# Two transformer blocks on one core: pulls joined, latent norms spread, combination weights in one tile, keys and first queries turned during dense work, and a last product with tokens on partitions

## The chip, the cores and the metric

The program runs on one core of a Trainium2 chip. The metric is the device time of one execution in microseconds (us), the median over several runs. TensorE (PE, with PEld for its weight loads), VectorE (DVE), ScalarE (ACT) and GpSimd (POOL) each take instructions in order from a queue of their own; SyncE (SP) issues most of the transfers.

## What is computed

512 tokens of width 1024 in float32 go through two kinds of block. The first block has two layers. A layer projects the normed input to twelve parts and mixes them three ways (latent attention, gated linear attention in chunks, retention in chunks), adds the output projection, and then a feed-forward part with a convolution over three tokens:

```
x = x + concat([y_a, y_b, y_c], axis=-1) @ w_out[l]
h = rmsnorm(x, ffn_norm[l]); u = h @ ffn_w_up[l]
x = x + (silu(causal_dwconv(a, ...)) * bv) @ ffn_w_down[l]
```

The second block has one layer with three branches: windowed attention in three dilated groups of eight heads, whose outputs are combined by a softmax over the groups' log-denominators; grouped-query attention with eight query heads and two key heads (RMS norm and rotation of queries and keys); and attention to 256 memory tokens. Each branch is gated, projected and merged, and the end is

```
out = merged @ w_out[layer]
x = x + rms_norm(out, g_post[layer])
```

## The kernel before

Features lie on partitions and tokens along the free axis (`x` is 128 x 8 x 512), so that a dense product is a sequence of matmuls with 512 token columns. For accuracy both operands of a dense product are split into a high and a low part (`split`, `split_weight`), and `mm3` issues three matmuls for one: high by high, high by low, low by high (lines 444 to 446). `dense` gives features on partitions (tile `ps`, 512 columns), `dense_tok` tokens on partitions (tile `pt`, 256 columns). Weights arrive in 326 pieces of up to 512 KB over SP's queue (`load`, three buffers), and each is split on ACT (line 424) and DVE (line 425), one piece ahead of its use.

The order of the work is set by a queue of generators, the class `Fill`. `fill.add` appends dense work; `f(us)`, that is `pull`, runs generators until about that many nominal us of dense work have been issued; `after(us, fn)` has a function run when so much more dense work has gone by; `settle` runs everything that is due or will be; `need(name)` runs the queue until that name is done. The pulls stand between the steps of an attention or mixing stage, so that PE has dense work while DVE and ACT prepare the next step. Their sizes stand in `PACE`. The tile framework's planner then places the instructions of each engine, so the trace does not follow the written order everywhere. PSUM has eight banks: three for dense work (`bank`) and five for all else (`mbank`). Most scratch tiles come from one ring of 43 buffers (`gt`).

The places that the change touches:

`later_rstd` computes the norms of the two latent projections (tiles `Rq`, `Rk`). `first` sums the squares through transposes and runs an inverse root of ten small DVE operations (`rsqrt`, line 500 its last); `second`, due `PACE["rank2"]` later, spreads the result over partitions by four small matmuls (`rows`, line 529). `uq_dense` calls `settle` before it reads them.

`gla` works through eight levels of block sizes (32, 16, 8, 4, 2, 1, 0, 64). At each level every head's small tiles of scores go into a PSUM bank of their own (tile `lv`, line 858, row groups of 32 and a column position of their own), with a pull after each of four token tiles; then ACT or DVE copies them on (`gD`, `gA`). `mix_out` multiplies the scores `A` with the values (tile `o`, line 912) and adds the state's part (line 907), for `gla` and for `ret`. `ret` makes its scores head by head (tile `rsc`, line 968), each followed by a DVE product (`rA`) and a pull.

In the second block `combine` turns the statistics of the three window groups (`stat`), makes the weights on DVE, puts a high and a low part into `cF`, turns it (tile `cf`, line 1425) and spreads it by matmuls (`cw`). `gqa_dense` projects and rotates queries (`bo`) and keys (`bk`, POOL line 1516); `gqa` then turns keys and queries on PE (`bkp`, `bqp`), splits them and runs the score loop (`bs`, line 1571). `finish` computes the last product with features on partitions, in two halves of 256 tokens, takes the norm over partitions through transposes (`tsq`) and row matmuls (`rows`), adds `x` and writes the output transposed; the host turns it back. A matmul in plain float32 leaves two records in the trace, a transpose one.

Of the kernel before, what the change touches and what calls it, by code (L numbers as in the profile page):

```python
# [17 lines left out]
S = 512  # L18
# [10 lines left out]
    rank2=6.0,  # L29
# [52 lines left out]
def weight_groups():  # L82
# [72 lines left out]
    two("out", "w_out_2", k8, _span(0, 1024))  # L155
# [180 lines left out]
class Prog:  # L336
# [74 lines left out]
    def split_weight(self, i):  # L411
# [362 lines left out]
    def gla(self, l, bc):  # L774
# [60 lines left out]
        for li, hs in enumerate(seq):  # L835
# [16 lines left out]
            for t in range(4):  # L852
# [7 lines left out]
                f(PACE["gla"])  # L860
# [36 lines left out]
    def mix_out(self, l, gkey, nkey, A, v, st, qg, bc, b0):  # L897
# [40 lines left out]
    def ret(self, l, bc, late, more):  # L938
# [185 lines left out]
    def run(self):  # L1124
# [11 lines left out]
        if self.stop:  # L1136
            nc.sync.dma_start(self.aps["out"].rearrange("(k p) t -> p k t", p=128), self.x)
            return
# [4 lines left out]
    def block2(self):  # L1143
# [14 lines left out]
        og, st = [], []  # L1158
        for gi in range(3):
# [22 lines left out]
        for i in range(4):  # L1182
            fill.add(("br", 2, i), self.branch(2, i, opm))
        fill.need()
# [97 lines left out]
    def window(self, gi):  # L1282
# [8 lines left out]
        st = self.cst1.tile([128, 4, 16], F32, name="stat", tag="stat", bufs=6)  # L1291
# [89 lines left out]
    def combine(self, og, st):  # L1381
        nc, T4, f = self.nc, self.T4, self.f
        scale = 64 ** -0.5
        for gi in (1, 2):
# [9 lines left out]
            st[gi] = self.cst1.tile([128, 4, 16], F32, name="stat", tag="stat", bufs=6)  # L1394
            nc.scalar.activation(st[gi], pb, AF.Copy)
# [345 lines left out]
```

## Time and profile before

| | us |
|---|---|
| median of 3 runs | 1990.25 (1987.42 to 1991.47) |
| profiled execution | 1990.08 |
| its span, first to last instruction | 1988.3 |
| PE busy in the span | 1954.8 (98%) |
| DVE busy | 1239.2 (62%) |
| ACT busy | 793.4 (40%) |
| POOL busy | 140.7 (7%) |

The profile is of one execution. An engine's busy time is the union of its instructions' spans. Matmuls are pipelined, so that a span reaches into the next one's: the time that a matmul adds is the distance from its start to the next start. The mean granted clock of TensorE is 0.993 of full speed.

### The profile page before, as it was taken

The page shows a single profiled execution, that of the slowest core. Times are in us where ns is not written, and L with a number is a line of the kernel's source. Part 1 is how long each engine was busy: PE and PEld are TensorE (multiplying, and loading weights), DVE is VectorE, ACT ScalarE, POOL GpSimd, SP SyncE. Part 2 cuts the span into 40 slices and gives each one's busy share as a digit, 9 for nine tenths or more (in the row PEclk, how much of TensorE's full clock was granted, in tenths as well). Part 3 has the DMA queues.
Part 4 walks back from the last instruction along what each step waited for, and adds up shares of the span by engine and source line. Part 5 has one row for each costly group of instructions (what it writes and reads, how often), then busy time and mean ns, then how long its engine had stood idle before and what let it go on. Part 6 is the DMA issues. An engine that isn't in the chain of part 4 may idle for free.

```text
span 1988.3 us, 28658 instructions
## 1 busy us (share of the span) xinstructions
PE 1954.8 (98%) x11351; PEld 1620.4 (81%) x11351; DVE 1239.2 (62%) x2299; ACT 793.4 (40%) x1473; POOL 140.7 (7%) x172
## 2 busy tenths in 40 slices
PE   9999999999999999999999999999999999999997
PEld 7879888888888878888888888887888877788887
DVE  6666576646556666576656466845456787655454
ACT  5545243222224635443222224525354456543242
POOL 1000000000000100000000000021131330000000
PEclk9999999999999999999999999999999999999998
DMA  5221123232323321133232334432222221123331
GB/s 196 60 80 44 64 89 101 84 109 85 106 80 107 94 67 50 41 96 95 93 90 96 103 113 123 135 109 67 75 75 67 75 64 54 63 67 98 101 96 54
DMA packets 55189, 172.30 MB, mean 87 GB/s; under 512 B 6494, under 2 KB 10096, under 8 KB 55056
## 3 DMA queue, kind: packets, MB, share of 16 engines
q1 hardware_dynamic: 53152, 165.47, 26.6%
q0 software_dynamic: 1760, 4.87, 0.9%
q8 instruction: 89, 1.46, 0.3%
q14 instruction: 44, 0.36, 0.1%
q10 hardware_dynamic: 144, 0.14, 0.0%
HBM read 167.05 MB, written 2.10 MB: 85 GB/s over the span
## 4 chain that ended last, share of the span: by engine, by line
PE 91%; DVE 5%; ACT 3%; issue 1%; POOL 0%; DMA 0%; DVEq 0%; POOLq 0%; ACTq 0%
PE ps L444 24%; PE ps L446 23%; PE ps L445 23%; PE pt L444 3%; PE pt L445 3%; PE pt L446 3%; PE o L912 2%; DVE wlo L425 1%; PE o L1029 1%; PE s L1006 1%; PE aq L1347 1%; PE bo L1596 1%; PE bpq L1584 1%; PE rows L529 1%; PE lv L858 1%
## 5 line engine op out<-in xcount | busy, mean ns | idle before, releaser
L424 ACT ACTIVATE whi<-wst 128x1024 fp32r<-128x1024 f32 (+3 forms) x318 | 316.3, 995 | 700.3 <-PE ps L445 566.4
L425 DVE TENSOR_TENSOR wlo<-wst,whi 128x1024 fp32r<-128x1024 f32 (+3 forms) x318 | 367.4, 1155 | 315.9 <-ACT whi L424 315.4
L444 PE MATMUL ps<-xh,whi 128*128 128x512 f32 (+1 forms) x1408 | 556.8, 396 | 0.0
L445 PE MATMUL ps<-xl,whi 128*128 128x512 f32 (+1 forms) x1408 | 550.3, 391 | 0.6 <-DVE xl L490 0.6
L446 PE MATMUL ps<-xh,wlo 128*128 128x512 f32 (+1 forms) x1408 | 549.8, 391 | 0.1
L444 PEld LDWEIGHTS ps<-xh,whi 128*128 128x128 f32 (+1 forms) x1408 | 264.4, 188 | 61.1 <-issue 6.7
L446 PEld LDWEIGHTS ps<-xh,wlo 128*128 128x128 f32 (+1 forms) x1408 | 264.3, 188 | 57.1 <-DVE wlo L425 0.9
L445 PEld LDWEIGHTS ps<-xl,whi 128*128 128x128 f32 (+1 forms) x1408 | 264.6, 188 | 55.8 <-DVE xl L490 2.8
L444 PE MATMUL pt<-whi,xh 128*128 128x256 f32 x480 | 143.2, 299 | 1.5 <-ACT bz L1523 0.8
L445 PE MATMUL pt<-wlo,xh 128*128 128x256 f32 x480 | 137.6, 287 | 0.0
L445 PE MATMUL ps<-fl,whi 128*128 128x512 f32 x352 | 137.0, 389 | 0.0
L444 PE MATMUL ps<-fh,whi 128*128 128x512 f32 x352 | 137.0, 389 | 0.0
L446 PE MATMUL ps<-fh,wlo 128*128 128x512 f32 x352 | 136.9, 389 | 0.0
L446 PE MATMUL pt<-whi,xl 128*128 128x256 f32 x480 | 136.5, 286 | 0.0
L444 PEld LDWEIGHTS pt<-whi,xh 128*128 128x128 f32 x480 | 92.7, 194 | 6.7 <-ACT bz L1523 1.3
L1067 DVE TENSOR_TENSOR x<-x,ps 128x512 f32<-128x512 f32 x96 | 65.7, 687 | 50.8 <-PE ps L446 50.6
L445 PEld LDWEIGHTS pt<-wlo,xh 128*128 128x128 f32 x480 | 93.3, 194 | 0.5 <-issue 0.2
L446 PEld LDWEIGHTS pt<-whi,xl 128*128 128x128 f32 x480 | 92.9, 194 | 0.2 <-issue 0.2
L445 PEld LDWEIGHTS ps<-fl,whi 128*128 128x128 f32 x352 | 66.1, 188 | 13.8
L446 PEld LDWEIGHTS ps<-fh,wlo 128*128 128x128 f32 x352 | 66.1, 188 | 13.7
L444 PEld LDWEIGHTS ps<-fh,whi 128*128 128x128 f32 x352 | 66.1, 188 | 13.6
L486 ACT ACTIVATE fh<-cv 128x512 fp32r<-128x512 f32 x44 | 27.9, 633 | 84.7 <-DVE cv L1121 84.7
(464 smaller groups left out, 2919.1 us busy)
## 6 DMA issues: line engine op xcount, KB each, us to landing
wst<-in_w SPq DMA_DIRECT2D x250, 512.0 KB, 3.5
wst<-in_w SPq DMA_DIRECT2D x54, 384.0 KB, 3.0
wst<-in_w SPq DMA_DIRECT2D x20, 256.0 KB, 2.6
x<-in_xT SPq DMA_DIRECT2D x8, 256.0 KB, 4.9
out<-out SPq DMA_DIRECT2D x8, 256.0 KB, 2.3
mt<-in_memT POOLq DMA_DIRECT2D x4, 256.0 KB, 4.1
c<-in_cst POOLq DMA_DIRECT2D x3, 256.0 KB, 3.5
s<-in_cst POOLq DMA_DIRECT2D x3, 256.0 KB, 2.9
```

The costliest lines, as they stand in the source:

```text
L424: nc.scalar.activation(hi, s3, AF.Copy)
L425: nc.vector.tensor_sub(lo, s3, hi.bitcast(F32))
L444: nc.tensor.matmul(out, lh, rh, start=start, stop=False, skip_group_check=True)
L445: nc.tensor.matmul(out, lh, rl, start=False, stop=False, skip_group_check=True)
L446: nc.tensor.matmul(out, ll, rh, start=False, stop=stop, skip_group_check=True)
L486: nc.scalar.activation(hi, src, AF.Copy)
L529: nc.tensor.matmul(ps[:, t, :], w, self.ident, start=True, stop=True)
L858: nc.tensor.matmul(ps[h][j0:j0 + w, t, c0:c0 + w], ke[hp, a:a + w], qe[hp, a + off:a + off + w], start=True, stop=True, tile_position=(32 ...
L912: nc.tensor.matmul(o[r, j, hd], A[h][:n, t, r], v[t][:n, hd], start=t + h == 0, stop=True, skip_group_check=True)
L1006: nc.tensor.matmul(s[:, :nk], qn[h][:, T4[qt]], kn[h][:, :nk], start=False, stop=True, skip_group_check=True)
L1029: nc.tensor.matmul(O[qt][:, h, :], PT[u][:, T4[kt]], v[kt][:, T4[h]], start=kt == 0, stop=kt == qt)
L1067: nc.vector.tensor_add(xm, xm, ps)
```

## The change

It has these parts. (1) The second step of the latent norms is due 11 instead of 6 us after the first. (2) In `gla` the four pulls of a level become one of four times the size, after all four token tiles; in `ret` the scores of the four heads go to four banks at once, token tile by token tile with the heads innermost, and the pulls are joined. (3) `mix_out` issues the state's products first, and each product of scores and values takes all 128 rows, for the left and the right 64 score columns in turn. (4) `combine` keeps the three groups in one tile and works on all at once. (5) Keys are doubled on POOL (each key head twice), turned and split from `gqa_dense`, 4 and 9 us of dense work later, and the first query pair 12 later; the others are turned from inside the score loop; four pulls of 0.88 at the head of `gqa` go. (6) The last product has tokens on partitions: 512 output features per matmul, the first half for four token tiles at once, the second tile by tile; the norm is then one value per partition. `x` is turned in place by `residual`, which stands in the queue between two steps of the last branch. The output is written as it is.

```diff
-    rank2=6.0,
+    rank2=11.0,
...
-    two("out", "w_out_2", k8, _span(0, 1024))
+    for i in range(2):
+        g.append(((2, "out", i), "w_out_2", 0, k8, _span(512 * i, 512)))
...
-            hi, lo = (TileList([self.gt(n, (128, 2, 256), F32R) for _ in range(2)], 2) for n in ("oh", "ol"))
-            for j in range(2):
-                self.split(hi.tiles[j], lo.tiles[j], s3[:, 2 * j:2 * j + 2])
+            hi, lo = ([self.gt(n, dtype=F32R) for _ in range(kt)] for n in ("oh", "ol"))
+            for j in range(kt):
+                self.split(hi[j], lo[j], s3[:, j])
...
-                f(PACE["gla"])
+            f(4 * PACE["gla"])
...
+            first = True
             for j in range(2):
                 t = 2 * tp + j
-                sl = slice(t * 128, t * 128 + 128)
                 if t:
-                    nc.tensor.matmul(o[:, j], qg[:, sl], st[t], start=j == 0, stop=True, skip_group_check=True)
+                    nc.tensor.matmul(o[:, j], qg[:, t * 128:t * 128 + 128], st[t], start=first, stop=True,
+                                     skip_group_check=True)
+                    first = False
+            for j in range(2):
+                t = 2 * tp + j
                 for h in range(4):
                     hd = slice(64 * h, 64 * h + 64)
-                    for n in (64, 128):
-                        r = slice(n - 64, n)
-                        nc.tensor.matmul(o[r, j, hd], A[h][:n, t, r], v[t][:n, hd], start=t + h == 0, stop=True,
+                    for r in (slice(0, 64), slice(64, 128)):
+                        nc.tensor.matmul(o[r, j, hd], A[h][:, t, r], v[t][:, hd], start=False, stop=True,
...
+        ps = [self.mbank("rsc", (128, 4, 128)) for _ in range(4)]
+        for t in range(4):
+            for h in range(4):
+                hp = slice(32 * h, 32 * h + 32)
+                nc.tensor.matmul(ps[h][:, t, :], rk[hp, T4[t]], rq[hp, T4[t]], start=True, stop=True)
         for h in range(4):
-            hp = slice(32 * h, 32 * h + 32)
-            ps = self.mbank("rsc", (128, 4, 128))
-            for t in range(4):
-                nc.tensor.matmul(ps[:, t, :], rk[hp, T4[t]], rq[hp, T4[t]], start=True, stop=True)
             a = self.gt("rA", (128, 4, 128))
-            nc.vector.tensor_mul(a, ps, rd[:, h:h + 1, :].to_broadcast([128, 4, 128]))
+            nc.vector.tensor_mul(a, ps[h], rd[:, h:h + 1, :].to_broadcast([128, 4, 128]))
             A.append(a)
-            f(PACE["ret2"])
+        f(4 * PACE["ret2"])
...
+            if i == 1:
+                fill.add("res", self.residual())
...
+        M, L = self.stats[:, :, :, :8], self.stats[:, :, :, 8:]
+        F = self.gt("cF", (128, 4, 4, 32))
+        nc.gpsimd.memset(F, 0.0)
+        E, W = (self.gt(n, (128, 4, 4, 8))[:, :3] for n in ("cE", "cW"))
         mx = self.small("cmx", (4, 8))
-        nc.vector.tensor_max(mx, st[0][:, :, :8], st[1][:, :, :8])
-        nc.vector.tensor_max(mx, mx, st[2][:, :, :8])
-        E = []
-        for gi in range(3):
-            e = self.small("ce", (4, 8))
-            nc.vector.tensor_sub(e, st[gi][:, :, :8], mx)
-            nc.scalar.activation(e, e, AF.Exp, scale=scale)
-            E.append(e)
+        nc.vector.tensor_max(mx, M[:, 0], M[:, 1])
+        nc.vector.tensor_max(mx, mx, M[:, 2])
+        nc.vector.tensor_sub(E, M, mx[:, None].to_broadcast([128, 3, 4, 8]))
+        nc.scalar.activation(E, E, AF.Exp, scale=scale)
+        f(PACE["com2"])
+        nc.vector.tensor_mul(W, E, L)
         den = self.small("cden", (4, 8))
-        f(PACE["com2"])
-        for gi in range(3):
-            t = den if gi == 0 else self.small("ct", (4, 8))
-            nc.vector.tensor_mul(t, E[gi], st[gi][:, :, 8:])
-            if gi:
-                nc.vector.tensor_add(den, den, t)
+        nc.vector.tensor_add(den, W[:, 0], W[:, 1])
+        nc.vector.tensor_add(den, den, W[:, 2])
         nc.vector.reciprocal(den, den)
-        F = self.gt("cF", (128, 4, 128))
-        nc.gpsimd.memset(F, 0.0)
-        for gi in range(3):
-            nc.vector.tensor_mul(E[gi], E[gi], den)
-            hi = self.spool.tile([128, 4, 8], F32R, name="ch", tag="ch", bufs=2)
-            nc.vector.tensor_copy(hi, E[gi])
-            nc.vector.tensor_copy(F[:, :, 32 * gi:32 * gi + 8], hi.bitcast(F32))
-            nc.vector.tensor_sub(F[:, :, 32 * gi + 8:32 * gi + 16], E[gi], hi.bitcast(F32))
+        nc.vector.tensor_mul(E, E, den[:, None].to_broadcast([128, 3, 4, 8]))
+        H = self.gt("cH", (128, 4, 4, 8), F32R)[:, :3]
+        nc.vector.tensor_copy(H, E)
+        Fg = F.rearrange("p t g d -> p g t d")
+        nc.vector.tensor_copy(Fg[:, :3, :, :8], H.bitcast(F32))
+        nc.vector.tensor_sub(Fg[:, :3, :, 8:16], E, H.bitcast(F32))
+        F = F.rearrange("p t g d -> p t (g d)")
         f(PACE["com3"])
...
+        kh, kl, qT = [], [], {}
+        kd = [self.gt("bkd", (128, 4, 2, 64)) for _ in range(2)]
+
+        def doubled():
+            for s in range(2):
+                nc.gpsimd.tensor_copy(kd[s], k[:, :, None, 64 * s:64 * s + 64].to_broadcast([128, 4, 2, 64]))
+
+        def keys():
+            for s in range(2):
+                pk = self.mbank("bkp")
+                for t in range(4):
+                    nc.tensor.transpose(pk[:, T4[t]], kd[s][:, t].rearrange("p w d -> p (w d)"), self.ident)
+                kh.append(self.gt("bkh", dtype=F32R))
+                kl.append(self.gt("bkl", dtype=F32R))
+                self.split(kh[s], kl[s], pk)
+
+        def queries(u):
+            qT[u] = [self.gt("bqT", dtype=F32R) for _ in range(2)]
+            pb = self.mbank("bqp")
+            for t in range(4):
+                nc.tensor.transpose(pb[:, T4[t]], q[u // 2][t // 2][:, t % 2, T4[u % 2]], self.ident)
+            self.stack(qT[u], pb)
+        self.fill.after(4.0, doubled)
+        self.fill.after(9.0, keys)
+        self.fill.after(12.0, lambda: queries(0))
+        self.z["b"] = kh, kl, qT, v, queries
...
-        pk = self.mbank("bkp")
-        for t in range(4):
-            nc.tensor.transpose(pk[:, T4[t]], k[:, t], self.ident)
-        kh = [self.gt("bkh", dtype=F32R) for _ in range(2)]
-        kl = [self.gt("bkl", dtype=F32R) for _ in range(2)]
-        for s in range(2):
-            a, b = slice(64 * s, 64 * s + 64), slice(64 - 64 * s, 128 - 64 * s)
-            nc.scalar.activation(kh[s][a], pk[a], AF.Copy)
-            nc.scalar.activation(kh[s][b], pk[a], AF.Copy)
-            nc.vector.tensor_sub(kl[s][a], pk[a], kh[s][a].bitcast(F32))
-            nc.vector.tensor_sub(kl[s][b], pk[a], kh[s][a].bitcast(F32))
-        qT = [[self.gt("bqT", dtype=F32R) for _ in range(2)] for _ in range(4)]
-        for u in range(4):
-            pb = self.mbank("bqp")
-            for t in range(4):
-                nc.tensor.transpose(pb[:, T4[t]], q[u // 2][t // 2][:, t % 2, T4[u % 2]], self.ident)
-            self.stack(qT[u], pb)
-            f(PACE["gqa1"])
...
+        def ahead(i, u):
+            if u[0] < 3 and u[1:] == (0, 2):
+                queries(u[0] + 1)
         units = [(pr, s, t) for pr in range(4) for s in range(2) for t in range(4)]
-        self.skew(units, ((0, score), (5, turn), (6, value)), PACE["gqa2"])
+        self.skew(units, ((0, ahead), (0, score), (5, turn), (6, value)), PACE["gqa2"])
...
+    def residual(self):
+        nc = self.nc
+        self.xt = self.x.rearrange("p (a b) s -> p a (b s)", b=2).rearrange("p a (t c) -> p a t c", t=4)
+        for kp in range(4):
+            ps = [self.mbank("xT", (128, 2, 2, 128)) for _ in range(2)]
+            for t in range(4):
+                for b in range(2):
+                    nc.tensor.transpose(ps[t // 2][:, t % 2, b], self.x[:, 2 * kp + b, self.T4[t]], self.ident)
+            for j in range(2):
+                nc.scalar.activation(self.xt[:, kp, 2 * j:2 * j + 2], ps[j].rearrange("p t b c -> p t (b c)"), AF.Copy)
+            yield 0.9
...
+        g = []
+        for c in range(2):
+            t = self.gt("gpost")
+            src = self.aps["gpost"]
+            nc.gpsimd.dma_start(t, bass.AP(tensor=src.tensor, offset=src.offset + 512 * c, ap=[[0, 128], [1, 512]]))
+            g.append(t)
         for k in range(8):
             self.split(self.xh[:, k], self.xl[:, k], self.merged[k], 0.5)
...
+        ss = self.small("oss", (4, 2))
+        y = {}
+
+        def ev(t, c, ps):
+            sq = self.gt("osq2")
+            nc.scalar.activation(sq, ps, AF.Square, accum_out=ss[:, t, c:c + 1])
+            y[t, c] = self.gt("oy2")
+            nc.vector.tensor_mul(y[t, c], ps, g[c])
+
+        ps = [self.bank("ps") for _ in range(3)] + [self.mbank("po")]
+        for k0, kt, hi, lo in self.weights((2, "out", 0)):
+            for k in range(kt):
+                for t in range(4):
+                    self.mm3(ps[t], self.xh[:, k0 + k, T4[t]], self.xl[:, k0 + k, T4[t]], hi[k], lo[k],
+                             k0 + k == 0, k0 + k == 7)
+        for t in range(4):
+            ev(t, 0, ps[t])
+        kept = list(self.weights((2, "out", 1)))
+        for t in range(4):
+            ps = self.mbank("po")
+            for k0, kt, hi, lo in kept:
+                for k in range(kt):
+                    self.mm3(ps, self.xh[:, k0 + k, T4[t]], self.xl[:, k0 + k, T4[t]], hi[k], lo[k],
+                             k0 + k == 0, k0 + k == 7)
+            ev(t, 1, ps)
+            v = self.small("ov", (1,))
+            nc.vector.tensor_reduce(v, ss[:, t], AX, OP.add)
+            r = self.rsqrt(v, "ort", (1,))
+            for c in (1, 0):
+                o = y[t, c].rearrange("p (a b) -> p a b", a=2)
+                nc.vector.scalar_tensor_tensor(o, o, r, self.xt[:, 2 * c:2 * c + 2, t], op0=OP.mult, op1=OP.add)
+                (nc.sync if c else nc.scalar).dma_start(self.aps["out"][T4[t], 512 * c:512 * c + 512], y[t, c])
```

## Rows read from the trace of the kernel before

**Rows 1.** The page, chain that ended last: shares by engine.
```profile
PE 91%; DVE 5%; ACT 3%; issue 1%; POOL 0%; DMA 0%; DVEq 0%; POOLq 0%; ACTq 0%
```

**Rows 2.** Timeline of PE: start us, span us, engine, line, operation, out<-in, shape, count.
```profile
1926.81 0.39 PE L445 MATMUL ps<-opl,whi 128*128 128x512 f32 x1
1927.04 0.39 PE L446 MATMUL ps<-oph,wlo 128*128 128x512 f32 x1
1927.26 0.28 PE L444 MATMUL ps<-xh,oh 128*128 128x256 f32 x1
1927.38 0.28 PE L445 MATMUL ps<-xl,oh 128*128 128x256 f32 x1
...
1974.57 0.28 PE L446 MATMUL ps<-xh,ol 128*128 128x256 f32 x1
```

**Rows 3.** Waits of PE: line, releaser, us in total, times, longest.
```profile
PE rows L529 <- DVE Rqt L500: 4.0, 2, 2.0
PE bs L1571 <- DVE bqT L762: 3.9, 1, 3.9
...
PE rows L529 <- DVE st L893: 2.4, 2, 1.2
PE cf L1425 <- DVE cF L1421: 2.1, 1, 2.1
```

**Rows 4.** Windows: us, busy of PE, PEld, DVE, ACT, POOL, granted clock, DMA.
```profile
45.00:122.30 77.30, 72.92 (x913) 58.85 (x911) 54.09 (x121) 39.26 (x86) 11.04 (x20) 0.98 0.24 69
660.00:740.00 80.00, 75.60 (x920) 61.23 (x918) 54.73 (x124) 38.97 (x85) 11.37 (x20) 0.96 0.24 72
1603.00:1619.00 16.00, 12.13 (x54) 9.73 (x53) 14.40 (x18) 7.36 (x13) 3.34 (x2) 0.79 0.39 125
```

**Rows 5.** Timeline of PE in mix_out, first call, first half.
```profile
122.36 1.61 PE L912 MATMUL o<-tv,gA 128*64 128x64 f32 x12 [0.16 <-ACT gA L863]
123.90 0.70 PE L907 MATMUL o<-st,qg 128*128 128x256 f32 x2
124.53 1.61 PE L912 MATMUL o<-tv,gA 64*64 64x64 f32 x12
126.07 0.50 PE L444 MATMUL ps<-ckh,whi 128*128 128x512 f32 x1
```

**Rows 6.** Timeline of PE at a value product of the window stage.
```profile
1542.12 1.09 PE L1369 MATMUL ao<-apt,av 128*64 128x128 f32 x16
1543.14 0.38 PE L444 MATMUL pt<-whi,xh 128*128 128x256 f32 x1
```

**Rows 7.** Timeline of PE at two groups of level tiles in gla.
```profile
50.76 0.75 PE L858 MATMUL lv<-qe,ke 32*32 32x32 f32 x64
51.44 0.50 PE L445 MATMUL ps<-xl,whi 128*128 128x512 f32 x1
...
86.12 0.37 PE L858 MATMUL lv<-qe,ke 32*64 32x64 f32 x16
86.42 0.39 PE L444 MATMUL pt<-whi,xh 128*128 128x256 f32 x1
```

**Rows 8.** Timeline of PE at retention scores.
```profile
202.66 1.71 PE L968 MATMUL rsc<-rT 32*128 32x128 f32 x16
204.30 0.39 PE L444 MATMUL pt<-whi,xh 128*128 128x256 f32 x1
```

**Rows 9.** Timeline of PE and DVE: query transposes, and the tail.
```profile
1607.06 1.03 PE L1558 MATMUL bqp<-c_ident,bo 128*128 128x128 f32 x8
1607.85 0.48 PE L444 MATMUL ps<-xh,whi 128*128 128x512 f32 x1
...
1979.06 1.20 PE L529 MATMUL rows<-c_ident,rt 128*128 128x128 f32 x4 [2.78 <-DVE rt L500]
1980.29 1.88 DVE L1700 TENSOR_TENSOR out<-out,rows 128x512 f32<-128x512 f32 x3 [1.38 <-PE rows L529]
```

**Rows 10.** Timeline of POOL at the end of the keys' rotation.
```profile
1579.67 1.28 POOL L1516 TENSOR_TENSOR bk<-bk,bsq 128x512 f32<-128x512 f32 x1 [0.26 <-DVE bsq L1514]
```

More of the change, by code (lines that the diff above doesn't have):

```diff
@@ L1136, in run @@
         if self.stop:
-            nc.sync.dma_start(self.aps["out"].rearrange("(k p) t -> p k t", p=128), self.x)
+            nc.sync.dma_start(self.aps["out"].rearrange("t (k p) -> p k t", p=128), self.x)
             return
@@ L1158, in block2 @@
         og, st = [], []
+        self.stats = self.cst1.tile([128, 3, 4, 16], F32, name="stats")
         for gi in range(3):
@@ L1290, in window @@
             og = [self.gt("og") for _ in range(4)]
-        st = self.cst1.tile([128, 4, 16], F32, name="stat", tag="stat", bufs=6)
+        st = self.stats[:, 0] if gi == 0 else self.cst1.tile([128, 4, 16], F32, name="stat", tag="stat", bufs=2)
         mx, sm = st[:, :, :8], st[:, :, 8:]
@@ L1393, in combine @@
                 nc.tensor.transpose(pb[:, t, :], r[:, T4[t]], self.ident[:16, :16])
-            st[gi] = self.cst1.tile([128, 4, 16], F32, name="stat", tag="stat", bufs=6)
-            nc.scalar.activation(st[gi], pb, AF.Copy)
+            nc.scalar.activation(self.stats[:, gi], pb, AF.Copy)
             f(PACE["com1"])
+        M, L = self.stats[:, :, :, :8], self.stats[:, :, :, 8:]
+        F = self.gt("cF", (128, 4, 4, 32))
+        nc.gpsimd.memset(F, 0.0)
+        E, W = (self.gt(n, (128, 4, 4, 8))[:, :3] for n in ("cE", "cW"))
@@ L1541, in gqa @@
         self.fill.settle()
[L1542 to L1560 removed]
+        kh, kl, qT, v, queries = self.z["b"]
         scale = 64 ** -0.5
@@ L1663, in cross @@
         return res
-    def finish(self):
-        nc = self.nc
+    def residual(self):
[9 more added lines that the diff above has]
+            yield 0.9
@@ L1667, in finish @@
+    def finish(self):
+        nc, T4 = self.nc, self.T4
+        g = []
[4 more added lines that the diff above has]
+            g.append(t)
         for k in range(8):
             self.split(self.xh[:, k], self.xl[:, k], self.merged[k], 0.5)
-        kept = {}
-        for half in range(2):
-            tk = slice(256 * half, 256 * half + 256)
-            acc = self.gt("acc")[:, :256]
-            out = [self.gt("out", (128, 2, 256)) for _ in range(4)]
-            for i in range(4):
-                if half == 0:
-                    kept[i] = list(self.weights((2, "out", i)))
-                ps = [self.bank("ps", (128, 256)) for _ in range(2)]
-                for k0, kt, hi, lo in kept[i]:
-                    for m in range(2):
-                        sl = slice(m * 128, m * 128 + 128)
-                        for k in range(kt):
-                            self.mm3(ps[m], hi[:, k, sl], lo[:, k, sl], self.xh[:, k0 + k, tk], self.xl[:, k0 + k, tk],
-                                     k0 + k == 0, k0 + k == 7)
-                for m in range(2):
-                    n = 2 * i + m
-                    if n == 0:
-                        nc.scalar.activation(acc, ps[m], AF.Square)
-                    else:
-                        q = self.gt("sq")[:, :256]
-                        nc.scalar.activation(q, ps[m], AF.Square)
-                        nc.vector.tensor_add(acc, acc, q)
-                    nc.scalar.activation(out[i][:, m], ps[m], AF.Copy, scale=self.vec("g_post_2", n))
-            v = self.tok_sums(acc, 1, 2)
-            nc.vector.tensor_scalar(v, v, 1.0 / D, EPS, op0=OP.mult, op1=OP.add)
-            r = self.rsqrt(v, "rt", (2, 1))
-            R = self.rows(r, 2)[:, :256]
-            dst = self.aps["out"].rearrange("(i k p) t -> i p k t", i=4, k=2)
-            for i in range(4):
-                o = out[i]
-                nc.vector.tensor_mul(o, o, R[:, None, :].to_broadcast([128, 2, 256]))
-                (nc.vector if i else nc.gpsimd).tensor_add(o, o, self.x[:, 2 * i:2 * i + 2, tk])
-                nc.sync.dma_start(dst[i][:, :, tk], o)
@@ L1716, in arrays_of @@
     a["qkn"] = np.stack([q, q[sw], k, k[sw]])
+    a["gpost"] = np.ascontiguousarray(inputs["g_post_2"])
     a["mla_out"] = np.ascontiguousarray(inputs["mla_out_norm"])
@@ L1735 @@
         aps[name] = nc.dram_tensor(f"in_{name}", a.shape, F32, kind="ExternalInput").ap()
-    aps["out"] = nc.dram_tensor("out_0", (D, S), F32, kind="ExternalOutput").ap()
+    aps["out"] = nc.dram_tensor("out_0", (S, D), F32, kind="ExternalOutput").ap()
     with tile.TileContext(nc) as tc:
@@ L1739 @@
     r = run_bass_kernel_spmd(nc, [{f"in_{k}": v for k, v in arrays.items()}], core_ids=[0])
-    return np.ascontiguousarray(r.results[0]["out_0"].T)[None]
+    return np.ascontiguousarray(r.results[0]["out_0"])[None]
```

2 lines of the change are left out of this document (removed).

## Prediction

> **What bounds the kernel now.** I read the chain of waits first: 91% of it is PE [rows 1]. PE's busy share says little beyond that, since a matmul's span overlaps its successor's; look at start-to-start times instead. A matmul of 512 columns starts 0.22 to 0.23 us after the one before it, one of 256 columns 0.12 [rows 2], though their own spans are 0.39 and 0.28. Time is won on PE in three ways: fewer or better packed starts, no wait in front of a start, no stretch at half clock. So I read next what PE waits for [rows 3], then the granted clock by stage [rows 4], and then the spacing inside each group of small matmuls that the diff touches [rows 5 to 8]. The dense work is a fixed sum: a pull that moves changes what it hides, not how much there is. The sum is made against the profiled execution's 1990.1 us (span 1988.3), 0.2 us from the median shown.
>
> **mix_out, full-height products.** Today products over 64 rows alternate with products over 128. Twenty-four of their records (a float32 matmul leaves two) and two state records fill 122.36 to 126.07; less the 0.63 between 123.90 and 124.53, that is 3.08 us, 0.128 each [rows 5]. Four token tiles, four heads, two halves and two records make 64 in each of four calls: 256 x 0.128 = 32.9 us. Afterwards all products have 128 rows and write the two column halves in turn. The nearest row is the window's value product, 128 rows by 64 columns in alternating halves: 16 records from 1542.12 to 1543.14, 0.064 each, with 128 moving columns where mix_out has 64 [rows 6]. So the bounds are 0.064 (gain 16.4) and half of it (gain 24.7). I take 21, nearer the middle, because the moving columns are halved and the weight load is not. That the narrower products of rows 5 lie farther apart than those of rows 6 is what a cost between two shapes looks like. [...]
>
> **gla, joined levels.** Sixteen small tiles take 0.30 us until dense work goes on (86.12 to 86.42); 64 in one go take 0.68 (50.76 to 51.44), 0.0107 each [rows 7]. So a split costs 0.30 - 16 x 0.0107 = 0.13 us beyond its tiles. The trace has 27 such groups a layer, where the new code makes eight: 19 x 2 x 0.13 = 5 as the low bound. The high bound is 11, a little over twice that, for the late start of the dense work on either side and for fragments of two to four tiles. I take 8. The level's DVE and ACT work is hidden by one stretch of 4 x 1.3 us of dense work instead of four of 1.3.
>
> **ret, four score banks.** The products of one head lie in the same 32 rows and run one by one: 16 records from 202.66 to 204.30, 0.10 each, 64 in all, 6.6 us [rows 8]. With heads innermost, neighbours lie in different rows. Bounds: 0.064 as in rows 6 (gain 2.5), or the spacing of rows 7 scaled from 32 to 128 columns, 0.043 (gain 3.9). I take 3.5. The four DVE products that follow now start together, under the joined 4 us of pulls.
>
> **rank2, 6 to 11.** PE waits 4.0 us for Rqt and, before the second norm's rows, 2.4 us behind the states' step on DVE, each once a layer and at most 2.0 [rows 3]. Five more us of dense work go ahead of the rows, more than the longest wait, so 6.4 go. [...] Bounds 6 and 11.1; I take 10. Nothing is late next: uq settles the queue before it reads either norm.
>
> **combine in one tile.** Some 23 small DVE operations become ten; PE waits 2.1 us for the last of them [rows 3]. Bounds 0 and 2.1; I take 1.5, since weight splits stay in DVE's queue.
>
> **Keys and first queries early.** The wait of 3.9 us before the first score goes [rows 3], and with it the slow stretch, 0.79 over 16 us, 3.4 us [rows 4]. Added are two POOL copies and four transposes, 0.4 us at 0.10 each (eight from 1607.06 to 1607.85 [rows 9]). POOL ends the rope of bk at 1580.95 and that operation takes 1.28 [rows 10]; two copies of that length end near 1583.5, while the key transposes come 9 us of dense work after the projection, near 1581. If they wait, all of PE's queue waits behind them, 0 to 2.6 us; I take 1.3. The later query turns ride in the score loop. Gain 3.9 + 3.4 - 0.4 - 1.3 = 5.6; bounds 1 (the copies are late and the clock falls all the same) and 7.
>
> **finish, tokens on partitions.** 384 matmuls of 256 columns run from 1927.26 to 1974.57, 47.3 us with the norm's products between them [rows 2]. 192 of 512 columns at 0.225 take 43.2: 4.1 gained. The tail from 1974.57 to 1988.3 is 13.7 us. From it go the row products, 1979.06 to 1980.29 (1.2), and six of eight DVE operations of 512 columns, three of which take 1.88 (3.8) [rows 9]; the root's chain and the last write stay: 5.0 gained. The residual is turned on PE: 32 transposes at 0.10, 3.2, and eight switches, 4 in all. Its eight ACT copies and the loads of g_post lie under dense work of the last branch and the first output half; without that cover the copies cost PE what ACT needs beyond the transposes, some 2. The weight splits of the second half run ahead under the first. Net 4.1 + 5.0 - 4 = 5.1; bounds 1 (copies and splits show) and 7.
>
> **Sum.** 21 + 8 + 3.5 + 10 + 1.5 + 5.6 + 5.1 = 54.7; 1990.1 - 54.7 = 1935.4 us. All low bounds (16.4, 5, 2.5, 6, 0, 1, 1) give 1958, all high ones (24.7, 11, 3.9, 11.1, 2.1, 7, 7) 1923.
>
> **Rivals.**
> One half at a time: if the column halves of mix_out don't run side by side, the spacing is twice that of rows 6, 0.128, which is today's; the 21 go, 1956. For it: both halves use all rows. Against: rows 6. Chance 0.12.
> Cover runs out: DVE or ACT come last in the mixing stages. DVE is busy 54.1 of 77.3 us in the first one [rows 4]; with 4 us less of small tiles and 5 less of waits and half clock there it is 54 of 68. If half of the 32.5 from mix_out, gla and ret comes back, 1952. For it: DVE's in-order queue already holds PE at both norms. Against: even 80% leaves room. Chance 0.2.
> The joins don't take: a planner places the instructions, and rows 7 show one level in one go where the code splits it. If it mixes in dense work all the same, the 8 and 3.5 go: 1947. Against: most groups follow the written pulls. Chance 0.1.
> Slower, by half clock: blocks of small tiles and 32 transposes in a row might let the clock fall. Half clock costs half of its stretch, so it must last 110 us to eat 54.7; with 120, 1995. For it: the mixing stages are long enough, and 0.79 over 16 us shows the price [rows 4]. Against: the stretches with a low clock are those of the long waits in rows 3, which go. Chance 0.05.
>
> **Chances.** The forecast has 0.5, the rivals 0.47 as given, and 0.03 is left for stalls that cancel the gain. A measurement of this kernel tells about 0.2% (4 us) from no change. Faster by more than that 0.92, within it 0.03, slower 0.05. The forecast's own range is 1923 to 1958; the first three rivals lie inside it, and for 8 in 10 I give 1918 to 1960.
>
> **What would show it.** Right: mix_out's records at 0.032 to 0.064 us; about eight groups of level tiles a layer; no PE wait for Rqt; the first key score without a wait and the clock at 1.00 there; 192 output matmuls at 0.225 and a tail near 9 us. Wrong: new PE waits for rA, gD or kd, mix_out at 0.128, or a clock below 0.95 over a whole stage.

## The result and the profile after

The changed kernel takes 1956.9 us (median of 4, 1956.7 to 1957.2), the kernel before 1989.5 on the same chip (1987.4 to 1991.5). The ratio is 0.9837, 95% interval 0.9819 to 0.9854: 1.6% faster, 32.5 us, of 54.7 forecast. Where experiments are compared below, their ratios to before are, with 0.1% as 2.0 us. Each ratio has an interval of 0.1 to 0.2% either side, so two experiments differ clearly only from about 4.5 us on; a smaller difference is argued from the profiles and not shown by the times. Plain medians can differ from the ratio by some us (`mix_out` alone: 17.9 by medians, 21.7 by the ratio).

The profiled execution has a span of 1955.3. Its chain of waits looks much as in [rows 1]:

```profile
PE 89%; DVE 6%; ACT 3%; issue 1%; POOL 0%; DMA 0%; DVEq 0%; ACTq 0%; POOLq 0%
```

The waits of PE (line, releaser, us in total, times, longest) answer to [rows 3]:

```profile
PE ps L445 <- DVE rt L769: 6.9, 2, 3.4
PE tsq L516 <- DVE cka L719: 3.8, 2, 1.9
PE lv L859 <- DVE st L894: 3.5, 2, 1.8
...
PE cf L1429 <- DVE cF L1424: 2.7, 1, 2.7
PE yt L1061 <- DVE st L894: 2.3, 2, 1.1
```

The waits for Rqt (4.0), st ahead of the rows (2.4) and bqT (3.9) are gone. In their place stand four new ones, 16.5 us together, and the one for cF has grown from 2.1 to 2.7. The timeline of PE at retention answers to [rows 5] and [rows 8]:

```profile
195.56 1.17 PE L972 MATMUL rsc<-rT 32*128 32x128 f32 x32
...
202.33 1.15 PE L916 MATMUL o<-tv,rA 128*64 128x64 f32 x32
```

A group's time holds the last record's own 0.27 or 0.22. So retention's scores lie (1.17 - 0.27)/31 = 0.029 us apart (0.10 before), mix_out's products (1.15 - 0.22)/31 = 0.030 there and 0.036 on the mean of all four calls (0.128 before). The granted clock (last but two of the columns) answers to [rows 4]:

```profile
78.00:96.00 18.00, 16.02 (x293) 15.15 (x292) 11.16 (x32) 4.76 (x9) 0.00 (x0) 0.81 0.12 32
...
116.00:126.00 10.00, 6.57 (x53) 4.60 (x52) 7.12 (x12) 5.35 (x10) 2.97 (x3) 0.83 0.38 114
...
1550.00:1560.00 10.00, 7.27 (x33) 5.99 (x31) 7.60 (x16) 2.77 (x5) 5.26 (x5) 0.86 0.31 105
```

Each of these three stretches lies at or behind one of the new waits: lv at 80.35, rt at 116.4, cF at 1554.7. The key score's stretch of 0.79 is at 1.00 now. Over a whole stage, 640 to 740, the clock is 0.93 (0.97 before).

Laid side by side at common points, the two timelines say where the 33.0 us of span come from. The last product of layer 1's output projection with the linear mixers' part starts at 883.0 before and at 855.7 after: 27.3 from the mixing stages (42.5 forecast). From there to the last window group's end nothing changes. From that to the last score of the grouped-query part it is 141.1 and 137.1 us; the four pulls of 0.88 that left `gqa`, 3.5 us of dense work, are done later, so combination, keys and queries gain 0.5 at most (7.1 forecast); counted, 18 dense matmuls of 0.226 us fewer stand there, 4.1 us, and nothing is gained. The rest, 5.2 to 5.8, is the finish (5.1 forecast). Such points are good to a few us: in the four kernels that are alike up to there (before, the finish alone, the combination alone, the keys alone) layer 1's mixing ends between 881.4 and 885.8, and in three that have all parts, among them the changed one, between 855.7 and 857.2.

### The profile page after: what moved, and what is told of

Same layout as the page of the kernel before. It is cut to its first block, busy times and chain, and to the rows that moved or that the text cites. A ratio compares the mean times of both kernels' runs of the same rounds, so it can differ in the third digit from the quotient of the medians.

```text
span 1955.3 us, 28303 instructions
## 1 busy us (share of the span) xinstructions
PE 1917.8 (98%) x11183; PEld 1594.2 (82%) x11183; DVE 1233.7 (63%) x2297; ACT 786.3 (40%) x1461; POOL 144.7 (7%) x174
## 4 chain that ended last, share of the span: by engine, by line
PE 89%; DVE 6%; ACT 3%; issue 1%; POOL 0%; DMA 0%; DVEq 0%; ACTq 0%; POOLq 0%
PE ps L445 23%; PE ps L447 23%; PE ps L446 23%; PE pt L445 3%; PE pt L447 3%; PE pt L446 3%; DVE wlo L426 1%; PE o L1034 1%; PE s L1011 1%; ACT whi L425 1%; PE aq L1355 1%; PE bo L1607 1%; PE bpq L1595 1%; PE rows L530 1%; PE o L916 1%
## 5 line engine op out<-in xcount | busy, mean ns | idle before, releaser
L446 PEld LDWEIGHTS ps<-fl,whi 128*128 128x128 f32 x352 | 66.1, 188 | 13.7
```

Of the source, the lines that this page charges most:

```text
L446: nc.tensor.matmul(out, lh, rl, start=False, stop=False, skip_group_check=True)
```

## The experiments

**One part alone, or undone.** First `mix_out` alone in the kernel before.

```diff
...
-                    for n in (64, 128):
-                        r = slice(n - 64, n)
-                        nc.tensor.matmul(o[r, j, hd], A[h][:n, t, r], v[t][:n, hd], start=t + h == 0, stop=True,
+                    for r in (slice(0, 64), slice(64, 128)):
+                        nc.tensor.matmul(o[r, j, hd], A[h][:, t, r], v[t][:, hd], start=False, stop=True,
...
```

> The kernel before with the full-height products of mix_out alone; gla's levels, ret, the norms, the combination, the keys and the finish stay as they were. In the trace after, these products lie 0.036 us apart where they lay 0.128: 256 x 0.092 = 23.6 us of TensorE's time, in four calls. Theory A (cover runs out): mix_out comes right behind the last level, whose ACT copies and DVE splits are already late there, so alone it gives well below 23.6, some 12 to 17 us (1973 to 1977), with a new wait ahead of the products of gla. Theory B (the joined levels or the later norms cost what is missing): mix_out alone gives its full 20 to 24 us (1966 to 1969). Theory C (the old alternation was hidden anyway): under 8 us.

Measured: 1969.1, ratio 0.9891 (0.9873 to 0.9908), 21.7 us (18 to 25 by the interval). Theory B; no wait of length arises ahead of gla's products. In its profile layer 1's mixing ends at 858.1, 24.9 earlier than before. Some 5 of that are lost again behind the combination, which the edit does not touch: there the clock falls behind the wait of 2.1 us for cF and stays low, where in the kernel before it stayed at 1.00 behind the same wait (windows of PE: us, busy, clock, DMA; the first fence is of the kernel before, where this wait ends at 1583.4, the second of `mix_out` alone, where it ends at 1558.5):

```profile
1580.00:1590.00 10.00, 7.87 (x36) 1.00 0.19 52
1590.00:1600.00 10.00, 10.00 (x38) 1.00 0.00 0
```
```profile
1550.00:1560.00 10.00, 7.87 (x36) 0.95 0.46 133
1560.00:1570.00 10.00, 10.00 (x24) 0.50 0.06 24
1570.00:1580.00 10.00, 10.00 (x21) 0.50 0.00 0
```

The five runs spread accordingly, from 1962.4 at a mean clock of 0.996 to 1970.5 at 0.989.

Next the norms' pull back at 6, and the levels split again.

```diff
-    rank2=11.0,
+    rank2=6.0,
```

> The changed kernel with the pull ahead of the latent norms' rows set back from 11 to 6. Theory A: the waits of the norms are only exchanged for others (tsq behind cka, lv behind the states' DVE work), so 1955 to 1959, and the waits for Rqt and st of the kernel before come back, 6 us, while others of that size go. Theory B, as forecast (10 us from this part): 1963 to 1967. Theory C: the later norms push DVE work into the end of gla and are the reason for the wait of 3.4 us for rt in each layer; then it is faster than the changed kernel, 1946 to 1951.

Measured: 1953.0, ratio 0.9815 (0.9800 to 0.9830): 4.4 us faster than the changed kernel, at the edge of what the intervals tell from nothing. That is none of the three sizes; the sign is theory C's, but its mechanism falls, for the wait for rt stays whole:

```profile
PE ps L445 <- DVE rt L769: 6.8, 2, 3.4
PE rows L530 <- DVE Rqt L501: 4.0, 2, 2.0
...
PE rows L530 <- DVE st L894: 2.4, 2, 1.2
```

So the waits are exchanged as theory A says, cka and lv (7.3) for Rqt and st (6.4). The rest goes with the clock: over 640 to 740 it is 0.93 with the change, 0.97 with the pull at 6 (the first of these rows is of the changed kernel), and layer 1 takes 3.2 us longer. In layer 0 it is 0.91 over 70 to 130 in both, and that layer's mixing ends at the same time (251.5 and 251.4). The later pull does not lower the clock by itself: with the pull at 11 and the levels split (below) it is 0.98 over 640 to 740.

```profile
640.00:740.00 100.00, 91.95 (x1069) 0.93 0.26 81
```
```profile
640.00:740.00 100.00, 92.57 (x1096) 0.97 0.27 81
```

```diff
-            f(4 * PACE["gla"])
+                f(PACE["gla"])
```

> The changed kernel with gla's levels pulled after each token tile again, 1.3 us four times in place of 5.2 once. Forecast for the join: 5 to 11 us, so 1962 to 1968. Theory A (cover runs out): the shorter TensorE time of joined levels is given back at new waits; splitting them again costs at most 3 us, 1957 to 1960, and the wait for rt at the end of gla shrinks. Theory C (the join hurts): faster than the changed kernel, under 1954.

Measured: 1958.5, ratio 0.9844 (0.9829 to 0.9859). The join is worth 1.4 us there, which can't be told from nothing. Without it the wait for rt is gone, and so is the one of 2.3 us for yt; the two longest that are left:

```profile
PE tsq L516 <- DVE cka L719: 3.8, 2, 1.9
PE lv L859 <- DVE st L894: 3.5, 2, 1.8
```

Theory A so far; the last experiment comes back to it. Then the finish alone, with the output's layout:

```diff
...
+            if i == 1:
+                fill.add("res", self.residual())
...
+        for k0, kt, hi, lo in self.weights((2, "out", 0)):
+            for k in range(kt):
+                for t in range(4):
+                    self.mm3(ps[t], self.xh[:, k0 + k, T4[t]], self.xl[:, k0 + k, T4[t]], hi[k], lo[k],
...
```

> The kernel before with the new finish alone: output projection with tokens on partitions, 512 columns, and the residual turned on TensorE under the last branch. Forecast for this part 5.1 us: 1984 to 1985. From the trace after: 47.3 less 43.4 us of output matmuls, a tail of 8.9 in place of 13.7, less 32 transposes at 0.109, which is 5.2. Rival: the residual and the weight splits show, and the part gives 1 us or less, as the distance from the last cross score to the end says (32.0 us gained there, 33.0 at the end); that distance holds dense work which the key part moved, so it is not a fair one by theory A.

Measured: 1983.0, ratio 0.9978 (0.9967 to 0.9989), 4.4 us (2 to 7). As forecast.

**The wait for rt.** Its chain in the changed kernel, from the timeline:

```profile
113.95 2.31 POOL L773 TENSOR_TENSOR qt<-rt,sw 128x512 f32<-128x512 f32 x1 [39.89 <-ACT whi L425]
...
116.30 1.28 ACT L762 ACTIVATE qr<-qt 64x512 fp32r<-64x512 f32 x2 [2.43 <-POOL qt L773]
...
116.96 1.41 DVE L763 TENSOR_TENSOR qr<-qt,qr 64x512 fp32r<-64x512 f32 x2 [1.83 <-ACT qr L762]
...
119.01 0.68 DVE L769 TENSOR_TENSOR rt<-ps,c 128x512 f32<-128x512 f32 x1
...
119.83 0.47 PE L445 MATMUL ps<-ckh,whi 128*128 128x512 f32 x1 [3.43 <-DVE rt L769]
```

PE wants the bank that the second rope has yet to read. The rope's two products on DVE (the second is L769) stand in its queue behind the first pair's stack (L763), which waits for ACT, which waits for the addition on POOL. In the kernel before the same chain ran at the same place and was in time: there small level tiles stand between these matmuls, and the second rope's last product ended at 120.3, before PE wanted the bank at 120.5.

```diff
-            self.rope64(t, ps, CR, SR)
+            self.rope64(t, ps, CR, SR, add=nc.vector)
...
-        nc.gpsimd.tensor_add(dst, a, b)
+        (add or nc.gpsimd).tensor_add(dst, a, b)
```

> The changed kernel with the last addition of the query rope (the one of uqr) on VectorE in place of GpSimd. In the trace after, that addition takes 2.31 and 2.15 us on GpSimd, each time beside a weight split of 1.2 us on VectorE, where before it took 1.28 and 1.30; the chain addition, stack, second rope ends in TensorE's wait of 3.4 us for rt in each layer, with matmuls at 0.43 behind it. Theory A (the stall hangs on this chain): an addition of about 0.7 us on VectorE takes 1.6 off each, the wait of 6.9 us in two layers goes or shrinks to under 2, and the half clock behind it too: 1946 to 1951. Theory B (the dense work there is used up, so that the next late buffer stops it): the wait is renamed, 1954 to 1958.

Measured: 1951.7, ratio 0.9816 (0.9803 to 0.9830), 4.2 us, again at the edge of what can be told; in the profile layer 1's mixing ends 5.9 us earlier. Theory A in part: the wait shrinks from 3.4 to 2.2 a layer, not under 1, and the stack (L763) in DVE's order ahead of the second rope's products keeps the rest:

```profile
112.88 0.69 DVE L773 TENSOR_TENSOR qt<-rt,sw 128x512 f32<-128x512 f32 x1
113.48 1.22 DVE L426 TENSOR_TENSOR wlo<-wst,whi 128x1024 fp32r<-128x1024 f32 x1
114.73 1.40 DVE L763 TENSOR_TENSOR qr<-qt,qr 64x512 fp32r<-64x512 f32 x2
116.17 0.69 DVE L768 TENSOR_TENSOR sw<-ps,s 128x512 f32<-128x512 f32 x1
116.78 0.68 DVE L769 TENSOR_TENSOR rt<-ps,c 128x512 f32<-128x512 f32 x1
```

**Combination and keys.** The doubled keys copied on ACT, then each part alone.

```diff
-                nc.gpsimd.tensor_copy(kd[s], k[:, :, None, 64 * s:64 * s + 64].to_broadcast([128, 4, 2, 64]))
+                nc.scalar.activation(kd[s], k[:, :, None, 64 * s:64 * s + 64].to_broadcast([128, 4, 2, 64]), AF.Copy)
```

> The changed kernel with the two copies of the doubled keys on ScalarE in place of GpSimd. Theory A: these copies and the rope's addition on GpSimd lengthen the combination's small VectorE operations beside them (1.34 us for 96 columns, 0.57 and 0.52 for 32, where the maxima of the same width take 0.18), so that TensorE waits 2.7 us for cF where it waited 2.1; only the copies leave, so 0.7 us off that wait, some 1 to 2 us in all with the half clock: 1954 to 1956. Theory B: the small operations wait for their semaphores and not for GpSimd; no change, 1956 to 1958, and they keep their lengths.

Measured: 1956.2, ratio 0.9837 (0.9822 to 0.9851), the time of the changed kernel. The wait for cF shrinks from 2.7 to 2.0, as theory A has it, but to no gain in the time that could be told. The DVE operation beside the copies (first fence, changed kernel) and without them (second):

```profile
1554.75 0.57 DVE L1416 TENSOR_TENSOR cden<-cW 128x32 f32<-128x32 f32 x1
```
```profile
1554.77 1.34 DVE L1414 TENSOR_TENSOR cW<-cE,stats 128x96 f32<-128x96 f32 x1
1556.14 0.19 DVE L1416 TENSOR_TENSOR cden<-cW 128x32 f32<-128x32 f32 x1
```

The 1.34 for 96 columns stays in both: it runs beside the keys' last addition on POOL, 2.28 us. What stands ahead of it, in the changed kernel:

```profile
1550.14 2.00 DVE L1518 TENSOR_TENSOR bsq<-bz,bt1s 128x128 f32<-128x128 f32 x4
1552.23 1.21 DVE L426 TENSOR_TENSOR wlo<-wst,whi 128x1024 fp32r<-128x1024 f32 x1
1552.31 2.28 POOL L1520 TENSOR_TENSOR bk<-bk,bsq 128x512 f32<-128x512 f32 x1 [0.26 <-DVE cE L1411]
1553.37 1.34 DVE L1414 TENSOR_TENSOR cW<-cE,stats 128x96 f32<-128x96 f32 x1
```

```diff
...
+            nc.scalar.activation(self.stats[:, gi], pb, AF.Copy)
...
+        nc.vector.tensor_sub(E, M, mx[:, None].to_broadcast([128, 3, 4, 8]))
...
```

> The kernel before with the combination in one tile alone. Forecast 1.5 us (bounds 0 and 2.1). Theory A: without the early keys there are no copies on GpSimd beside it, and the wait of 2.1 us for cF shrinks to under 1: 1 to 2 us faster than before, 0.999 to 0.9995. Theory B (the part itself is worth nothing; a weight split sits in VectorE's queue ahead of it either way): the wait stays at 2 to 3 us and the time is that of before or 1 us over it.

Measured: 1991.9, ratio 1.0015 (1.0005 to 1.0025), 3.0 us slower. Theory B: the wait for cF is 2.0 where it was 2.1. The 3 us go with the clock again, behind that wait:

```profile
1580.00:1590.00 10.00, 7.97 (x24) 0.67 0.19 52
1590.00:1600.00 10.00, 10.00 (x23) 0.50 0.00 0
1600.00:1610.00 10.00, 10.00 (x23) 0.50 0.14 52
```

Its twelve runs range from 1985.5 at a mean clock of 0.996 to 1994.7 at 0.989. At 0.996 the kernel before takes 1985.4 to 1987.4: as far as the one run at that clock shows, the part without the low stretch is worth nothing in either direction. Why the stretch comes in most of its runs is not shown.

```diff
-        self.z["b"] = q, k, v
...
+        self.fill.after(4.0, doubled)
+        self.fill.after(9.0, keys)
+        self.fill.after(12.0, lambda: queries(0))
+        self.z["b"] = kh, kl, qT, v, queries
```

> The kernel before with the early keys and first queries alone. Forecast 5.6 us. From the traces: the wait of 3.9 us for bqT is gone after, but the key transposes run at 0.21 apart at half clock behind the wait for cF, and new waits of 1.5 us stand in the score loop; from the first wait for cF to the last score the change gained 5.4 us, of which 3.5 is dense work that only moves (four pulls of 0.88). Theory A: 1.5 to 3.5 us, 0.9982 to 0.9992. Theory B: what was lost there came from the combination beside it, and alone it gives the full 5 to 6 us, 0.997.

Measured: 1988.9, ratio 1.0002 (0.9992 to 1.0011), nothing. Neither theory's size: the wait for bqT is gone, and in its place the one for cF is 3.0 instead of 2.1 and the score loop's turns wait too:

```profile
PE cf L1425 <- DVE cF L1421: 3.0, 1, 3.0
PE bpq L1591 <- DVE bmx L1581: 0.9, 1, 0.9
PE bpq L1591 <- ACT bp L1583: 0.4, 1, 0.4
```

Against before the waits of this stage fall by 1.7 us (6.0 to 4.3), and the clock, 0.84 over 1580 to 1590 where 0.66 stood over 1610 to 1620, gives back about 1.7. With four transposes more some 3 us should be left; why none shows is open. That the combination beside it spoils its gain is refuted.

**Repairs.** The rope's addition on DVE, the stack later, and the norms' pull at 8:

```diff
-    rank2=11.0,
+    rank2=8.0,
...
-            self.rope64(t, ps, CR, SR)
-            self.stack(qr[2 * m:2 * m + 2], t)
+            self.rope64(t, ps, CR, SR, add=nc.vector)
+            self.fill.after(2.6, lambda: self.stack(qr[2 * m:2 * m + 2], t))
...
```

> The changed kernel with the pull ahead of the norms' rows at 8 in place of 11, the last addition of uqr's rope on VectorE, and the stack of each pair of query heads 2.6 us of dense work later, so that the second rope's two products, which free TensorE's bank, don't queue behind it. Theory A: with the addition alone the wait for rt fell from 3.4 to 2.2 us a layer; it was the stack in VectorE's order that kept the rest, so now it falls under 0.5, and the norm's pull at 8 leaves neither the wait for Rqt (2.0) nor that for cka (1.9) above 1: 1944 to 1949. Theory B (waits only change their names): a wait of 2 us stays in each layer at either place, 1950 to 1953.

Measured: 1949.3, ratio 0.9807 (0.9787 to 0.9827). The wait for rt is gone, one of 1.3 a layer for kn takes its place, and at 8 the wait for Rqt is 2.0 a layer, as at 6: theory A for the stack, B for the norm.

```diff
-    com3=3.0,
+    com3=6.0,
```

> The changed kernel with the pull ahead of the combination's transposes at 6 in place of 3 us. Dense work is a fixed sum, so only the wait can change. Theory A: the wait of 2.7 us for cF goes and the half clock of 1550 to 1562 with it: 4 to 5 us faster than the changed kernel, 1951 to 1953. Theory B: the keys' transposes, which now come first, wait for the copies on GpSimd in its place: 1955 to 1957.

Measured: 1956.0, ratio 0.9836 (0.9819 to 0.9852), no gain: theory B. The waits only change places:

```profile
PE bpq L1595 <- ACT bp L1587: 2.0, 1, 2.0
...
PE cf L1429 <- DVE cF L1424: 0.9, 1, 0.9
...
PE bkp L1551 <- POOL bkd L1545: 0.6, 1, 0.6
```

All together, with the norms' pull at 6:

```diff
-    rank2=11.0,
+    rank2=6.0,
...
-    com3=3.0,
+    com3=6.0,
...
-            self.rope64(t, ps, CR, SR)
-            self.stack(qr[2 * m:2 * m + 2], t)
+            self.rope64(t, ps, CR, SR, add=nc.vector)
+            self.fill.after(2.6, lambda: self.stack(qr[2 * m:2 * m + 2], t))
...
```

> The changed kernel with the norms' pull back at 6, the rope's addition on VectorE with the stack later, and 6 us of dense work ahead of the combination's transposes. Theory A, the single gains add up: 3.7 for the pull, 5 to 9 for the rope's chain, 4 for the combination, so 1940 to 1946. Theory B (the same dense work can hide only one of them): 1947 to 1952.

Measured: 1944.3 (1943.2 to 1947.0), ratio 0.9781 (0.9764 to 0.9797). Theory A in its number, and the fastest kernel here: 11 us faster than the changed one. Not in all its terms: the 4 us for the combination did not come alone (above), and here nearly all of the gain lies ahead of it: layer 1's mixing ends at 842.7 instead of 855.7, 13.1 of the 13.9 us between the profiles. So the rope's chain and the norms' pull made it. The clock over 640 to 740 and the largest waits:

```profile
640.00:740.00 100.00, 94.32 (x1146) 1.00 0.27 82
```
```profile
PE rows L530 <- DVE Rqt L501: 4.0, 2, 2.0
...
PE ps L445 <- DVE kn L750: 2.5, 2, 1.3
PE rows L530 <- DVE st L894: 2.4, 2, 1.2
```

Last, the same with the levels split again:

```diff
-            f(4 * PACE["gla"])
+                f(PACE["gla"])
```

> The run with all repairs, its levels of gla split into four pulls of 1.3 us again. In the changed kernel the join was worth 1.5 us (1956.9 against 1958.5), and the split kernel had no wait for rt, which is 6.9 us with the join. Theory A (the join saves its 8 us on TensorE, and the rope's stall took them back): with the stall nearly gone the join is worth 5 to 8, so the split run takes 1949 to 1953. Theory B (the join itself is worth little, since split pulls cost TensorE hardly anything): 1944 to 1947.

Measured: 1951.6, ratio 0.9811 (0.9797 to 0.9824). Theory A: with the rope's stall repaired the join is worth 0.30%, 6 us (7.1 at the end of layer 1's mixing, 849.7 against 842.7), where with the stall it was worth 1.4. The norms' pull is at 6 in this pair and at 11 in the other.

## Why the prediction was right or wrong

**mix_out.** Right in size, and in that the spacing makes it: 21 forecast, 21.7 measured alone. The interval allows 18 to 25, and layer 1's mixing ends 24.9 earlier. The spacing is 0.036, near the lower bound of 0.032, and 256 x 0.092 makes 23.6; 0.036 holds the first products of gla in each layer, 32 records in 1.76 and 1.64 us at a granted clock of 0.60 and 0.65, while in ret, at 1.00, they lie 0.030 apart. Their weight loads last 0.138 us each, all hold all 128 rows, and the products' starts lie 0.030 apart: a load runs beside other products. The rival "one half at a time" is refuted.

**gla's levels.** The saving on PE was right: 8 forecast, 6 measured once the stall was out of the way. What failed is the cover: "the level's DVE and ACT work is hidden by one stretch". In the changed kernel PE reached the second query projection's bank before its rope had read it and waited 6.9 us, so that 1.4 were left. This is the rival "cover runs out" in kind, not in extent: the forecast saw it as half of 32.5 us, spread over the mixing stages; the runs put it on one chain of DVE, ACT and POOL, and mix_out alone kept its whole gain. That the stall needs the join was shown: with the levels split it is gone, although mix_out and ret are as in the changed kernel.

**ret.** Forecast 3.5. From rows: 64 records went from 6.6 us to 1.9, 4.7 and more than the high bound of 3.9, since 0.029 apart is closer than the 0.043 that was taken for the least. The new wait of 2.3 for yt, behind the states' step on DVE, stands in this stage, but it is gone when gla's levels are split (twice, at either pull of the norms), so it is not ret's alone. ret was not run alone; what the other runs leave for it is 4.1 (below), good to a few us.

**rank2.** The step that failed: 10 forecast, 4.4 lost; the loss is at the edge of what the times tell, but 10, or the low bound of 6, is out. "Nothing is late next" was wrong. The norms' late step was one link of a queue on DVE; given 5 us more, PE met the next two links, cka and the states' step ahead of lv, 7.3 us for the 6.4 saved, and in layer 1 the clock fell farther. The forecast's 10 holds 3.6 us beyond the 6.4 of waits, set for the clock; no run shows this term: over 640 to 740 the clock is 0.93 with the change, 0.97 before. The fall came with the stall for rt beside the later pull (0.98 without the stall, 0.97 with the stall and the pull at 6). The later pull alone in the kernel before was not run.

**Combination.** 1.5 forecast, nothing or a loss measured. From the timeline, the cost lay not in the number of operations: they are held by what stands ahead of them on DVE (the rope's products, 2.00; a weight split, 1.21) and by POOL beside it (0.57 for 32 columns beside the keys' copies, 0.19 without them). No run took the first two away. "Some 23 small DVE operations become ten" was true but for one (they become eleven) and off the path.

**Keys and queries.** 5.6 forecast, nothing measured. The wait for bqT went, as stated, but 2.7 us of wait for cF, keys turned at a granted clock of 0.50 (1558.3 to 1560.2; 0.21 apart, 0.10 expected) and 1.5 us of new waits in the score loop came. Two steps failed: the slow stretch did not go, it moved to cF, and by the timeline the later query turns did not ride along for nothing. The copies on POOL took 0.58 each, not 1.28, and PE did not wait for them itself (but 0.6 us in the run with the longer pull); they cost it 0.7 by way of DVE's small operations (cF, 2.7 against 2.0 with the copies on ACT).

**finish.** 5.1 forecast, 4.4 measured. From rows: the output matmuls take 43.4 (43.2 forecast), the tail 8.9 from 13.7, the residual's transposes lie 0.109 apart (0.10).

**Clock.** That "the stretches with a low clock are those of the long waits in rows 3, which go" failed: the waits came back elsewhere, and their clock with them (0.993 before, 0.992 after). Of the forecast's signs of being wrong one came clearly, a clock below 0.95 over a whole stage (0.93 over 640 to 740). The rival "slower, by half clock" was far off in extent.

**The sum.** The measured 1956.9 lies inside the forecast's 1923 to 1958, but only just, and partly by luck: the joined levels (1.4), rank2 (-4.4), the combination (-3.0) and the keys (-0.4) all came in under their low bounds, and mix_out and the finish, above theirs, made up for it. That the number is the one of the rival "one half at a time" (1956) is chance, for that rival is refuted. By points in the profiles 33.0 of the 54.7 came: 15.2 are missing in the mixing stages, 6.6 or a little more at combination and keys. At the end of layer 1's mixing (883.0 before) mix_out alone is 24.9 early; from the changed kernel (855.7) the split levels take off 1.5 (857.2) and the pull at 6 adds 3.2 (852.5); that leaves 27.3 - 24.9 - 1.5 + 3.2 = 4.1 for ret, a remainder that no run checks. By the ratios, alone or undone, the parts make 21.7 + 1.4 + 4.1 - 4.4 - 3.0 - 0.4 + 4.4 = 23.8 of 32.5. The gap of 8.7 is no larger than what the intervals of these terms, added in squares, allow (about 9). The long low stretch behind the combination, which the profiles of two parts alone have and the changed kernel's has not, may be some 5 of it; how it divides is not settled.

## What to carry to other kernels

Where PE is the bound and the rest only just keeps up, a saving on PE stands where nothing is queued close behind it (mix_out, the finish) and can be taken back where another engine's chain comes due (the joined levels); price a pull by what is next in DVE's queue, not by the wait that it removes. When a stall appears, follow its releaser back in the timeline: here one addition on another engine and a stack issued later freed most of what the join had saved. A part with fewer instructions need not gain anything when its last one still waits behind the same neighbours (the combination). And when parts are added up, check which of them make the total: here it came out within the range while four of seven parts did not.

## What was not expected of the hardware

POOL's addition of the query rope took 1.29 us in the kernel before and 2.23 after, with nothing changed in it (first fence before, second after; ns, least, median, most):

```profile
L772 POOL TENSOR_TENSOR qt<-rt,sw x4: 1285/1293/1300, 114.9 to 739.0; 128x512 f32<-128x512 f32 x4
```
```profile
L773 POOL TENSOR_TENSOR qt<-rt,sw x4: 2149/2234/2317, 114.0 to 724.7; 128x512 f32<-128x512 f32 x4
```

After, a weight split on DVE (1.2 us, two operands) runs beside each; before, in layer 0, copies out of PSUM or, but for its last 0.3 us, nothing did. At 113.95 and 120.42 the addition starts with 1.18 and 1.02 us of a split still to run, which with 1.29 makes 2.47 and 2.31, and it took 2.31 and 2.15. So it lost 1.02 and 0.86 us, an estimate from these times: nearly all that the split ran beside it. What the two share was not shown. It cuts the other way too: DVE's operation of 32 columns took 0.57 beside POOL's copies and 0.19 without them.

And the clock: in the second block, behind a wait of 2.0 to 2.1 us for cF it stayed at 1.00 in the profile of the kernel before and fell to 0.50 for over 20 us in two others. Executions of one kernel differ by up to 9 us with it (1985.4 at a mean clock of 0.996, 1994.1 at 0.991 for the kernel before); the kernel with all repairs, at 0.997 to 0.999, spreads over 4.
